# Five dense products by Strassen's scheme in a decoder layer that splits fp32 in two float32r parts

## The chip, the cores and the metric

The kernel runs on one core of one Trainium2 chip, as one launch. The metric is the device time of a run in microseconds (us). TensorE is called PE, VectorE DVE, ScalarE ACT, GpSimd POOL; SP issues most of the loads. Each engine takes its instructions from a queue of its own, in order: one that waits holds up all that stand behind it.

## What is computed

One layer for 512 tokens of width 1024. A combined input projection feeds two groups of heads, an SSD scan and a retention; their outputs go through one output projection, and a norm, a cross-attention into 256 memory tokens and a gated feed-forward part follow. Cut to the products that the change touches:

```
z, xbc, dt, q, k, v, g = split(x @ w_in)           # v: 1024 -> 1024
y_ret = silu(g) * groupnorm(retention(q, k, v))
y_ssd = rmsnorm(ssd(xbc, dt) * silu(z))
x1 = LN(alpha * x  + concat(y_ssd, y_ret) @ w_mix_out)   # 2048 -> 1024
x2 = LN(alpha * x1 + cross_attention(x1, mem))
a, u = split(causal_conv(x2 @ w_ffn_up + b))
y = LN(alpha * x2 + (silu(a) * u) @ w_ffn_down)          # 2752 -> 1024
```

## The kernel before

**Numbers.** Every fp32 operand is split in two float32r parts: h is a cast, l is the rest. A product of two tiles is three matmuls, h·h, h·l and l·h (`mm3`, line 104), which add into one bank of PSUM (128x512). The side of the tokens is kept split in SBUF; the weights come as a stream.

**The stream of weights.** `Stream` hands out 157 groups of 128x1024 in the order of their use. For each, SP loads `raw` (L124), ACT casts it to `wh` (L126) and DVE subtracts to get `wl` (L128); for 12 groups (60 to 67 and 92 to 95, `POOL_L`) POOL does the subtraction. Four pairs of `wh` and `wl` and three `raw` are in rotation, so a group is made ready while those ahead of it are used.

**The dense products.** `tok` makes 512 tokens x 512 columns: four banks, one for each 128 tokens, and each group of weights serves 24 matmuls (2 blocks of 128 rows, 4 token tiles, 3 matmuls). A product of 1024 x 1024 is two such calls, 8 groups, 192 matmuls. `feat` makes the transposed form, 128 columns x 512 tokens, also 24 matmuls to a group.

**What sets the order.** PE's instructions are pinned in the order in which the code writes them (`pin`). Small work (the chunks of the scans, norms, transposes) is written as generators that yield, and `weave` puts a few dense matmuls between its steps. The instructions of the other engines are ordered by a scheduler when the kernel is built.

**Places that the change touches.**
- The input stage: products for q, k and v; each q or k bank is turned by `rotary` (DVE multiplies at L275 and L276, POOL adds at L280 and L281). The chain for dt (`dt_chain`) is woven in.
- The gates: eight `feat` products give the retention's gate (`gate`), then two `tok` products give z (`z_gate`), where POOL multiplies (L626), takes the root of the norm (L629 to L631) and DVE scales (L632) the SSD output X[t].
- Output projection: first the retention half, with the transposes of X[t] (`ssd_out`, L108) woven in, then the SSD half, with the first norm behind it. `into_acc` adds each bank to the accumulator `acc` (L649, L651), which four POOL DMAs (L642) load with x.
- Feed-forward: tiles i of 128 columns; a pair of tiles gives one block k of the hidden product (L906), which ACT and DVE split (L908, L909). After tiles 16, 32 and 43 a part of the down projection follows: k 0 to 7, 8 to 15, then the rest.

SBUF holds tiles in several pools: `s` (20 slots of 4 KB a partition), `x`, `acc` and `row`.

Of the kernel before, what the change touches and what calls it, by code (L numbers as in the profile page):

```python
# [13 lines left out]
P = 128  # L14
T = 512
# [32 lines left out]
# columns of the parameter array  # L48
# [5 lines left out]
def tile_layer(ctx, tc, wst, wdt, xt, xn, memt, rows, small_row, par, cst, mdec, out):  # L54
# [38 lines left out]
    # The tensor engine runs its instructions in the order in which they are written here.  # L93
# [9 lines left out]
    def mmul(o, lhsT, rhs, start=True, stop=True):  # L103
        pin(nc.tensor.matmul(o, lhsT=lhsT, rhs=rhs, start=start, stop=stop))  # L104
# [6 lines left out]
    class Stream:  # L111
        def __init__(self):
            self.n = 0
            self.i = 0
            self.q = []
            self.total = wst.shape[0]

        def push(self, parts=1, between=None):
            r = ring.tile([P, 1024], F32, tag="raw", name=nm("raw"), bufs=RAW)
            h = ring.tile([P, 1024], F32R, tag="wh", name=nm("wh"))  # L120
            l = ring.tile([P, 1024], F32R, tag="wl", name=nm("wl"))
            for i in range(parts):
# [33 lines left out]
    def mm3(o, a, b, start, stop):  # L156
        mmul(o, a[0], b[0], start, False)
        mmul(o, a[0], b[1], False, False)
        mmul(o, a[1], b[0], False, stop)
# [28 lines left out]

    def drain(*gens):
        for g in gens:  # L190
            for _ in g:
                pass
# [9 lines left out]

# [1 line left out]
    xT = [slot("x", [P, 4, T], F32R) for _ in range(4)]  # L204

    def xk(k):
        return xT[k // 4][:, k % 4, :], xT[2 + k // 4][:, k % 4, :]
# [5 lines left out]
    for j in range(4):  # L213
        r = big([P, 1024])
        rv = r.rearrange("p (k t) -> p k t", k=2)
        xv = xt[j].rearrange("p (k t) -> p k t", k=2)
        h = xT[j // 2][:, 2 * (j % 2):2 * (j % 2) + 2, :]
        l = xT[2 + j // 2][:, 2 * (j % 2):2 * (j % 2) + 2, :]
# [32 lines left out]
    def bcast_row(src):  # L251
        r = slot("row", [P, 1024], F32, 2)
# [31 lines left out]
    def v_done(n):  # L284
        def done(t, b):
            (nc.scalar.copy if t % 2 else nc.vector.tensor_copy)(out=V[t][:, n * 512:(n + 1) * 512], in_=b)
        return done
# [20 lines left out]
    def dt_chain():  # L308
# [40 lines left out]
        # The differences of the running sums between two positions come from the tensor engine.  # L349
        # Four heads take 32 rows: the sums in two parts against ones, and ones against minus the sums.  # L350
# [6 lines left out]
        w = slot("acc", [P, 2, 512], F32R)  # L357
# [6 lines left out]
    dense = seq(tok(x_lhs, all8, NT, rotary(1)), *[tok(x_lhs, all8, NT, v_done(n)) for n in range(2)])  # L364
# [4 lines left out]
    maskdec = slot("row", [P, 8, P], F32, 2)  # L369
# [140 lines left out]
    def prepare(c):  # L510
        xdt = slot("acc", [P, 1024], F32)
# [8 lines left out]
    def ssd():  # L520
# [4 lines left out]
        for c in range(NT):  # L525
# [3 lines left out]
            if c < NT - 1:  # L529
                xde = slot("acc", [P, 1024], F32)  # L530
# [10 lines left out]
            def seg(q):  # L541
# [4 lines left out]
                # at or before a position the difference is at most 0; the others fall to cb's mask  # L546
# [58 lines left out]

    yret = [None] * 8

    def gate(j):
        def done(b):
# [4 lines left out]
            stt(out=sg, in0=sg, scalar=0.5, in1=y, op0=mult, op1=mult)  # L614
            yr = big([P, 2, T], F32R)
            nc.scalar.copy(out=yr[:, 0, :], in_=sg)
            tt(out=yr[:, 1, :], in0=sg, in1=f(yr[:, 0, :]), op=sub)
            yret[j] = yr
        return done

# [16 lines left out]
    drain(dense)  # L637
    drain(tok(x_lhs, all8, NT, z_gate(1)))

    acc = [slot("acc", [P, 1024], F32) for _ in range(NT)]  # L640
# [12 lines left out]

# [55 lines left out]
    def ssd_lhs(k, t):  # L709
        return yssd[t][:, 0, k, :], yssd[t][:, 1, k, :]  # L710
# [366 lines left out]
```

## Time and profile before

| | |
|---|---|
| median of 3 runs | 956.35 us (956.29 to 956.6) |
| span of the profiled execution | 953.9 us, 11550 instructions |
| its own time | the span is what the profile gives of it; 956.35 − 953.9 = 2.45 us of the median lie outside a span |
| PE | 944.3 us busy, 99% of the span |
| DVE | 563.6 us, 59% |
| ACT | 340.9 us, 36% |
| POOL | 140.0 us, 15% |
| chain of work that ended last | PE 97%, of it the dense matmuls (L104) 95% of the span and the transposes (L108) 3% |

The page is read from two sides. The busy shares say which engine has no room; the chain of work that ended last says whether that engine also sets the end, or whether it waits for others in between. Here both name PE. Durations of matmuls in a timeline are those of pipelined work (0.39 us for one of 128x512, though a new one starts each 0.23 us), so the pace is read from the distance of starts. The granted clock of TensorE is 1.00 in nearly the whole span, which is its upper level, 2.4 GHz; the lower is 1.2 GHz.

### The profile page before, as it was taken

Reading aid. Unit: us, or ns where it says so; the run is one execution under the profiler, and the core shown is the slowest. Engines: PE = TensorE matmul, PEld = TensorE weight load, DVE = VectorE, ACT = ScalarE, POOL = GpSimd, SP = SyncE. Lnnn points to the kernel's source line nnn. Section 1 sums busy time; section 2 is a strip of 40 time slices with the busy share of each in tenths; the row PEclk is TensorE's granted clock in tenths of the full one; section 3 lists DMA queues with packets and bytes.
Section 4 is the critical chain, followed back from the end, with each engine's and each line's share of the span. In section 5 each row is a group of like instructions: output and inputs, shape, how many; then the busy total and the mean of one; then the engine's idle time right before and its main releaser. Section 6 shows DMA issues by size and latency. Waiting matters only on the chain.

```text
span 953.9 us, 11550 instructions
## 1 busy us (share of the span) xinstructions
PE 944.3 (99%) x4607; PEld 776.5 (81%) x4607; DVE 563.6 (59%) x847; ACT 340.9 (36%) x487; POOL 140.0 (15%) x150
## 2 busy tenths in 40 slices
PE   9999999999999999999999999999999999999996
PEld 6788877788777888889888888988888888888874
DVE  5652566687765463448645668766535566336577
ACT  4122333345443431223533413544323443224420
POOL 1330110014252530065000006000000000000003
PEclk9999999999999999999999999999999999999999
DMA  8233211222211262425621112432322323323202
GB/s 296 87 115 103 67 45 67 67 89 67 67 45 67 89 221 88 154 89 176 221 88 47 67 66 89 136 108 88 98 101 89 111 89 95 103 89 110 89 22 89
DMA packets 26981, 95.24 MB, mean 100 GB/s; under 512 B 3120, under 2 KB 3632, under 8 KB 26928
## 3 DMA queue, kind: packets, MB, share of 16 engines
q1 hardware_dynamic: 25056, 88.09, 27.7%
q0 software_dynamic: 1728, 6.29, 1.9%
q8 instruction: 36, 0.59, 0.3%
q14 instruction: 17, 0.14, 0.1%
q10 hardware_dynamic: 144, 0.13, 0.0%
HBM read 92.41 MB, written 2.10 MB: 99 GB/s over the span
## 4 chain that ended last, share of the span: by engine, by line
PE 97%; DVE 1%; DMA 1%; SPq 0%; issue 0%; ACT 0%; DVEq 0%
PE b L104 95%; PE b L108 3%; DMA raw<-in_wst 1%; DVE acc L699 0%; DVE acc L692 0%; DVE x L153 0%; SPq L221 0%; DVE wl L128 0%; DVE acc L857 0%; DVE st L687 0%; ACT wh L126 0%; SPq L124 0%; DVEq L1073 0%; DVE st L688 0%
## 5 line engine op out<-in xcount | busy, mean ns | idle before, releaser
L104 PE MATMUL b<-x,wh 128*128 128x512 f32 (+1 forms) x1200 | 359.1, 382 | 0.5 <-DVE x L153 0.5
L128 DVE TENSOR_TENSOR wl<-raw,wh 128x1024 fp32r<-128x1024 f32 (+1 forms) x146 | 179.9, 1234 | 225.9 <-ACT wh L126 225.3
L126 ACT CAST wh<-raw 128x1024 fp32r<-128x1024 f32 (+1 forms) x157 | 164.8, 1050 | 311.5 <-PE b L104 275.1
L104 PEld LDWEIGHTS b<-x,wh 128*128 128x128 f32 x1200 | 218.2, 188 | 45.0 <-issue 4.2
L104 PE MATMUL b<-x,wl 128*128 128x512 f32 (+1 forms) x600 | 227.1, 378 | 0.0
L104 PE MATMUL b<-wh,s 128*128 128x512 f32 (+2 forms) x680 | 214.1, 391 | 0.0
L104 PE MATMUL b<-wh,x 128*128 128x512 f32 x512 | 163.2, 395 | 0.0
L104 PEld LDWEIGHTS b<-wh,s 128*128 128x128 f32 (+1 forms) x680 | 127.3, 188 | 30.7 <-issue 5.1
L104 PE MATMUL b<-wl,s 128*128 128x512 f32 (+1 forms) x340 | 131.5, 387 | 0.0
L104 PEld LDWEIGHTS b<-x,wl 128*128 128x128 f32 x600 | 112.9, 188 | 21.3
L104 PEld LDWEIGHTS b<-wh,x 128*128 128x128 f32 x512 | 96.0, 188 | 23.6 <-issue 2.2
L104 PE MATMUL b<-wl,x 128*128 128x512 f32 x256 | 99.9, 390 | 0.7 <-DVE wl L128 0.7
L104 PEld LDWEIGHTS b<-wl,s 128*128 128x128 f32 x340 | 63.9, 188 | 12.2
L257 POOL TENSOR_TENSOR st<-st,epst 128x1 f32<-128x1 f32 (+1 forms) x16 | 3.1, 192 | 479.6 <-DVE st L688 479.2
L894 DVE SCALAR_TENSOR_TENSOR t<-b,pr,t 128x511 f32<-128x511 f32 x86 | 64.1, 746 | 1.4
L104 PEld LDWEIGHTS b<-wl,x 128*128 128x128 f32 x256 | 48.1, 188 | 11.4 <-DVE wl L128 1.1
L128 POOL TENSOR_TENSOR wl<-raw,wh 128x1024 fp32r<-128x1024 f32 x12 | 34.8, 2916 | 68.5 <-ACT wh L126 68.5
L892 ACT ACTIVATE t<-b,cw,pr 128x512 f32<-128x512 f32 x43 | 33.3, 775 | 0.0
L908 ACT CAST s<-t 128x512 fp32r<-128x512 f32 (+1 forms) x22 | 13.6, 620 | 54.3 <-DVE t L906 54.3
L897 ACT ACTIVATE t<-t 128x512 f32<-128x512 f32 x21 | 13.3, 632 | 42.2 <-DVE t L895 42.2
L649 DVE TENSOR_TENSOR acc<-acc,b 128x512 f32<-128x512 f32 x24 | 15.8, 678 | 17.9 <-PE b L104 17.9
L104 PE MATMUL b<-s,wh 128*128 128x256 f32 x128 | 23.4, 285 | 0.0
(166 smaller groups left out, 856.3 us busy)
## 6 DMA issues: line engine op xcount, KB each, us to landing
raw<-in_wst SPq DMA_DIRECT2D x156, 512.0 KB, 3.3
row<-in_rows POOLq DMA_DIRECT2D x7, 512.0 KB, 6.2
acc<-in_xn POOLq DMA_DIRECT2D x4, 512.0 KB, 6.4
s<-in_xt SPq DMA_DIRECT2D x3, 512.0 KB, 7.7
out_y<-acc SPq DMA_DIRECT2D x3, 512.0 KB, 2.6
raw<-in_memt SPq DMA_DIRECT2D x2, 512.0 KB, 3.3
raw<-in_wst SPq DMA_DIRECT2D x2, 256.0 KB, 3.3
s<-in_xt SPq DMA_DIRECT2D x2, 256.0 KB, 4.3
```

The costliest lines, as they stand in the source:

```text
L104: pin(nc.tensor.matmul(o, lhsT=lhsT, rhs=rhs, start=start, stop=stop))
L108: pin(nc.tensor.transpose(o, i, ident[:p, :p]))
L126: copy(out=h[:, c], in_=r[:, c])
L128: sub_l(out=l[:, c], in0=r[:, c], in1=f(h[:, c]), op=sub)
L257: gtt(out=o, in0=v, in1=epst[:, :n], op=add)
L649: tt(out=a, in0=a, in1=b, op=add)
L892: nc.scalar.activation(out=c, in_=u, func=AF.Identity, bias=cw[0][:, i:i + 1], scale=ffp[:, i, 2:3])
L894: stt(out=c[:, d:], in0=u[:, :T - d], scalar=ffp[:, i, 2 - d:3 - d], in1=c[:, d:], op0=mult, op1=add)
L897: nc.scalar.activation(out=c, in_=c, func=AF.Silu)
L908: nc.scalar.copy(out=hd[:n, 0, :], in_=ca[:n, :])
```

## The change

Five products of 1024 x 1024 become Strassen's scheme (in Winograd's form): the values of the retention, the two halves of the output projection, and the down projection for k 0 to 7 and k 8 to 15. Tokens, inner blocks and columns are halved; instead of eight products of quarters there are seven, in the order m1, m2, m6, m5, m7, m3, m4. Each takes two groups of weights and 24 matmuls.

- **Weights.** `Quarters` has 8 loaded blocks (11, 12, 21, 22, two of each) and 14 groups to split: 11, 21, T2, T1, T3, 22, T4. The T's are sums of quarters, which POOL makes: 8 adds of 128x1024 a product (L172 to L175). Each group then serves 12 matmuls, not 24. The quarters are loaded into `s` tiles, up to 4 groups further ahead, and not before PE has reached the place of that `get`.
- **Tokens.** `sides` makes S1 to S4 with 8 POOL adds of 128x512 a product (L303; 4 of 128x1024 for the SSD half) and splits them (ACT L297, DVE L298).
- **Sums of the result.** m1, m6, m7 and m4 add up in the same two banks (`u`), m5 and m3 in two others; `done` adds a bank to `acc` after every product: 14 adds of 128x512, not 8. A bank that goes on must have been read first.
- **Moved.** `ssd_out` yields 2 ahead of its first transposes, not 4. The down projection's parts come after tiles 18, 34 and 43. `gate` no longer splits its output, `ff_done` no longer splits blocks k 0 to 15; `sides` does.
- All SBUF tiles of 4 KB come from one set `s` with 37 slots. The weights are laid out by quarters on the host.

The core of the diff:

```diff
+        ORDER = ("11", "21", "T2", "T1", "T3", "22", "T4")
+        def load(self):
+            for q in {"11": ("11",), "21": ("21",), "T2": ("12", "22")}.get(self.what, ()):
+                t = big([P, 1024])
+                d = nc.sync.dma_start(out=t, in_=wst[self.of.n + self.PLACE[q + self.k]])
+                tc.add_manual_dep(d.ins, last_pe[0].ins.name, ..., reason="not before its time")
...
+            if self.what == "T2":
+                t2_ = raw_slot()
+                add_(out=b11, in0=b12, in1=b11, op=sub)
+                add_(out=t2_, in0=b22, in1=b11, op=sub)
+                add_(out=b21, in0=b21, in1=t2_, op=sub)
+                add_(out=b12, in0=b22, in1=b12, op=sub)
...
+            h, l = pair()
+            nc.scalar.copy(out=h, in_=src)
+            tt(out=l, in0=src, in1=f(h), op=sub)
...
+    def strassen(side, done):
+        bk = {}
+        for m, a, where, start in ((1, "11", "u", True), (2, "12", "b", True), (6, "S2", "u", False),
+                                   (5, "S1", "c", True), (7, "S3", "u", False), (3, "S4", "c", False),
+                                   (4, "22", "u", False)):
+            if start:
+                bk[where] = [bank() for _ in range(2)]
+            for kp in range(2):
+                wh, wl = W.get(2)
+                for t in range(2):
+                    for j in range(2):
+                        k = 2 * kp + j
+                        mm3(bk[where][t], side(a, k, t), (wh[:, j, :], wl[:, j, :]), start and k == 0, k == 3, not start)
+                    if kp == 1:
+                        done(m, t, bk[where][t])
+                    yield
...
+        comb(a22, a21, a22, add)
+        comb(a21, a11, a21, sub)
+        comb(a11, a22, a11, sub)
+        split("S2", a11)
+        split("S1", a22)
+        comb(a12, a12, a11, sub)
+        split("S3", a21)
+        split("S4", a12)
...
-    dense = seq(*[tok(tok2(yret), all8, NT, into_acc(n, ALPHA)) for n in range(2)])
+    dense = strassen(ret_side, acc_quarter(ALPHA))
...
-    for i1, ks in ((16, list(range(8))), (32, list(range(8, 16))), (43, [16, 17])):
+    for n, i1 in enumerate((18, 34, 43)):
...
+        if n < 2:
+            drain(strassen(hid_side[n], acc_quarter(None if n else ALPHA)))
```

Three places show how the order moves. **POOL where the retention half of the output projection begins**, before: the second `z_gate` product's multiplies (L626) follow the small ones of the first.

```order
L631 TENSOR_SCALAR st_2439<-st_2439 128x1
L629 TENSOR_SCALAR st_2456<-st_2455 128x1
L630 TENSOR_TENSOR st_2456<-st_2456,mhalf 128x1
L631 TENSOR_SCALAR st_2456<-st_2456 128x1
L626 TENSOR_TENSOR s_793<-s_793,t_443_2568 128x512
L626 TENSOR_TENSOR s_794<-s_794,t_446_2585 128x512
L629 TENSOR_SCALAR st_2573<-st_2572 128x1
L630 TENSOR_TENSOR st_2573<-st_2573,mhalf 128x1
```

After: three of the eight side sums (L303, of 128x2x256) and the T2 sums of the first weights (L172 to L175) stand there; `s_843` is X[0], whose multiply is now L775.

```order
L303 TENSOR_TENSOR s_837<-s_837,s_836 128x2x256
L303 TENSOR_TENSOR s_838<-s_839,s_838 128x2x256
L303 TENSOR_TENSOR s_839<-s_839,s_838 128x2x256
L172 TENSOR_TENSOR s_2288<-s_2580,s_2288 128x1024
L173 TENSOR_TENSOR raw_2758<-s_2582,s_2288 128x1024
L175 TENSOR_TENSOR s_2580<-s_2582,s_2580 128x1024
L174 TENSOR_TENSOR s_2413<-s_2413,raw_2758 128x1024
L775 TENSOR_TENSOR s_843<-s_843,t_478_2654 128x512
L172 TENSOR_TENSOR s_2344<-s_2612,s_2344 128x1024
L778 TENSOR_SCALAR st_2659<-st_2658 128x1
L775 TENSOR_TENSOR s_844<-s_844,t_481_2671 128x512
L779 TENSOR_TENSOR st_2659<-st_2659,mhalf 128x1
```

Twelve big adds now stand ahead of the first multiply of X[0]'s second half, and two more ahead of the root (L778 to L780) that X[0] needs behind it.

**POOL between the rotary sums of q and those of k**, before (L280, L281 the rotary sums, L341 a step of the chain for dt):

```order
L280 TENSOR_TENSOR s_150<-t_50_291,t_51_292 128x8x32
L281 TENSOR_TENSOR s_150<-t_51_292,t_50_291 128x8x32
L341 TENSOR_TENSOR t_63_378<-av,cs 128x512
L280 TENSOR_TENSOR s_147<-t_73_464,t_74_465 128x8x32
L281 TENSOR_TENSOR s_147<-t_74_465,t_73_464 128x8x32
L280 TENSOR_TENSOR s_148<-t_75_476,t_76_477 128x8x32
L281 TENSOR_TENSOR s_148<-t_76_477,t_75_476 128x8x32
```

After (L424 and L425 are the rotary sums, L488 is the step for dt):

```order
L424 TENSOR_TENSOR s_154<-t_57_301,t_58_302 128x8x32
L425 TENSOR_TENSOR s_154<-t_58_302,t_57_301 128x8x32
L172 TENSOR_TENSOR s_187<-s_436,s_187 128x1024
L173 TENSOR_TENSOR raw_591<-s_438,s_187 128x1024
L175 TENSOR_TENSOR s_436<-s_438,s_436 128x1024
L488 TENSOR_TENSOR t_79_422<-av,cs 128x512
L172 TENSOR_TENSOR s_219<-s_468,s_219 128x1024
L173 TENSOR_TENSOR raw_616<-s_470,s_219 128x1024
L175 TENSOR_TENSOR s_468<-s_470,s_468 128x1024
L174 TENSOR_TENSOR s_251<-s_251,raw_591 128x1024
L424 TENSOR_TENSOR s_151<-t_90_510,t_91_511 128x8x32
```

Seven T adds for the values' weights stand between them now, and eight side sums ahead of q's.

**DVE at the last hidden block ahead of the first down part**, before (L906 the hidden product, L909 its split, L128 weight splits):

```order
L895 TENSOR_TENSOR t_905_5453<-t_905_5453,fix 128x2
L906 TENSOR_TENSOR t_900_5416<-t_900_5416,t_905_5453 128x512
L909 TENSOR_TENSOR s_5459<-t_900_5416,s_5459 128x512
L128 TENSOR_TENSOR wl_5498<-raw_5496,wh_5497 128x1024
L128 TENSOR_TENSOR wl_5528<-raw_5526,wh_5527 128x1024
```

After (L1072 the hidden product, L298 splits of side sums, L181 a weight split):

```order
L1057 TENSOR_TENSOR t_983_5614<-t_983_5614,fix 128x2
L298 TENSOR_TENSOR s_5645<-s_5101,s_5644 128x512
L1072 TENSOR_TENSOR s_5540<-t_977_5575,t_983_5614 128x512
L298 TENSOR_TENSOR s_5651<-s_5385,s_5650 128x512
L298 TENSOR_TENSOR s_5659<-s_5101,s_5658 128x512
L298 TENSOR_TENSOR s_5627<-s_5540,s_5626 128x512
L298 TENSOR_TENSOR s_5633<-s_5540,s_5632 128x512
L298 TENSOR_TENSOR s_5665<-s_5385,s_5664 128x512
L1056 SCALAR_TENSOR_TENSOR t_1003_5703<-b_5678,pr,t_1003_5703 128x511
L181 TENSOR_TENSOR wl_5710<-s_5502,wh_5709 128x1024
```

The split of a side sum, the first L298 here, stands ahead of the hidden product, and six such splits ahead of the next weight split.

## Rows read from the trace of the kernel before

**Rows 1.** The page: busy time of the engines, and the chain that ended last.
```profile
PE 944.3 (99%) x4607; PEld 776.5 (81%) x4607; DVE 563.6 (59%) x847; ACT 340.9 (36%) x487; POOL 140.0 (15%) x150
...
PE 97%; DVE 1%; DMA 1%; SPq 0%; issue 0%; ACT 0%; DVEq 0%
```

**Rows 2.** Timeline of ACT, 389 to 402 us (start, us, engine, line).
```profile
389.59 1.05 ACT L126 CAST wh<-raw 128x1024 fp32r<-128x1024 f32 x1 [4.38 <-PE b L104]
...
395.03 1.05 ACT L126 CAST wh<-raw 128x1024 fp32r<-128x1024 f32 x1 [3.43 <-PE b L104]
```

**Rows 3.** Groups by line and shape, all engines (count | busy us, mean ns | idle before).
```profile
L128 DVE TENSOR_TENSOR wl<-raw,wh 128x1024 fp32r<-128x1024 f32 x144 | 178.5, 1242 | 225.3 <-ACT wh L126 224.7
L126 ACT CAST wh<-raw 128x1024 fp32r<-128x1024 f32 x156 | 164.2, 1053 | 307.9 <-PE b L104 275.1 <-DMA raw<-in_wst 21.7 <-issue 6.2
...
L651 DVE SCALAR_TENSOR_TENSOR acc<-acc,b 128x512 f32<-128x512 f32 x24 | 16.1, 684 | 6.2 <-PE b L104 6.2
...
L909 DVE TENSOR_TENSOR s<-t,s 128x512 fp32r<-128x512 f32 x21 | 14.5, 692 | 13.0 <-ACT s L908 13.0
```

**Rows 4.** Timeline of POOL, 405 to 430 us.
```profile
407.04 2.39 POOL L128 TENSOR_TENSOR wl<-raw,wh 128x1024 fp32r<-128x1024 f32 x1 [61.79 <-ACT wh L126]
...
423.35 6.22 POOL L128 TENSOR_TENSOR wl<-raw,wh 128x1024 fp32r<-128x1024 f32 x2 [0.22 <-ACT wh L126]
```

**Rows 5.** Timeline of DVE, 422 to 431 us.
```profile
422.70 1.28 DVE L699 SCALAR_TENSOR_TENSOR acc<-acc,st,row 128x1024 f32<-128x1024 f32 x1
423.89 3.43 DVE L692 SCALAR_TENSOR_TENSOR acc<-acc,st,row 128x1024 f32<-128x1024 f32 x1
427.25 0.68 DVE L687 BATCH_NORM_STATS2 st<-acc 128x6 f32<-128x512 f32 x1
427.85 2.81 DVE L699 SCALAR_TENSOR_TENSOR acc<-acc,st,row 128x1024 f32<-128x1024 f32 x1
```

**Rows 6.** Timeline of POOL, 15 to 61 us.
```profile
19.02 0.30 POOL L881 TENSOR_TENSOR cw<-cw,pr 128x43 f32<-128x43 f32 x1
...
30.73 1.74 POOL L281 TENSOR_TENSOR s<-t,t 128x256 f32<-128x256 f32 x1
...
53.11 0.74 POOL L280 TENSOR_TENSOR s<-t,t 128x256 f32<-128x256 f32 x1 [8.20 <-DVE t L276]
```

**Rows 7.** Timeline of DVE, 29 to 31 us.
```profile
30.06 0.68 DVE L276 TENSOR_TENSOR t<-b,cs 128x512 f32<-128x512 f32 x1
30.66 1.21 DVE L128 TENSOR_TENSOR wl<-raw,wh 128x1024 fp32r<-128x1024 f32 x1
```

**Rows 8.** Timeline of POOL, 304 to 345 us.
```profile
312.80 1.28 POOL L626 TENSOR_TENSOR s<-s,t 128x512 f32<-128x512 f32 x1
...
315.74 2.19 POOL L626 TENSOR_TENSOR s<-s,t 128x512 f32<-128x512 f32 x1 [1.47 <-DVE t L603]
...
337.04 2.20 POOL L626 TENSOR_TENSOR s<-s,t 128x512 f32<-128x512 f32 x1 [1.47 <-DVE t L603]
...
342.02 2.20 POOL L642 DMA_DIRECT2D acc<-in_xn  x4
```

**Rows 9.** Timeline of DVE, 336 to 339 us.
```profile
336.87 1.22 DVE L128 TENSOR_TENSOR wl<-raw,wh 128x1024 fp32r<-128x1024 f32 x1
```

**Rows 10.** Timeline of PE, 330 to 337 us.
```profile
331.35 0.39 PE L104 MATMUL b<-wh,s 128*128 128x512 f32 x1
...
336.80 0.38 PE L108 MATMUL b<-cs,s 128*128 128x128 f32 x2
```

**Rows 11.** Landing of the acc loads (line L642, us to landing).
```profile
DMA to landing us min/median/max: 3.6/6.4/10.0
```

**Rows 12.** Timeline of PE, first 6 us.
```profile
1.18 4.02 PE L149 MATMUL b<-t 128*128 128x512 bf16 x9 [1.18 <-DVE t L146]
```

**Rows 13.** Windows after the last matmul (PE, PEld, DVE, ACT, POOL busy, PEclk, DMA, GB/s).
```profile
947.00:949.00 2.00, 0.00 (x0) 0.00 (x0) 1.90 (x5) 0.00 (x0) 0.97 (x2) 1.00 0.60 244
951.00:952.00 1.00, 0.00 (x0) 0.00 (x0) 0.00 (x0) 0.00 (x0) 0.00 (x0) 0.50 1.02 361
```

More of the change, by code (lines that the diff above doesn't have):

```diff
@@ L189, in drain, with by_pairs, raw @@
+    def by_pairs(r):
+        def raw(i, j):
+            return [r[2 * j + n][:, :, 256 * i:256 * i + 256] for n in range(2)]
+        return raw
     def drain(*gens):
@@ L282, in rotary, with v_quarter @@
         return done
[L284 to L287, printed above, removed]
+    def v_quarter(m, t, b):
+        t0, n, first = GOES[m]
+        v = V[t0 + t][:, n * 512:(n + 1) * 512]
+        if first:
+            nc.scalar.copy(out=v, in_=b)
+        else:
+            tt(out=v, in0=v, in1=b, op=add)
     all8 = list(range(KD))
@@ L356, in dt_chain @@
         tt(out=cl, in0=b, in1=f(ch), op=sub)
-        w = slot("acc", [P, 2, 512], F32R)
+        w = big([P, 2, 512], F32R)
         for i in range(2):
@@ L362, in dt_chain, with x_quarter, k_and_v @@
         seg_w.append(w)
-    dense = seq(tok(x_lhs, all8, NT, rotary(1)), *[tok(x_lhs, all8, NT, v_done(n)) for n in range(2)])
+    def x_quarter(i, j):
+        return lambda k, t: x_lhs(4 * j + k, 2 * i + t)
+    def k_and_v():
+        yield from tok(x_lhs, all8, NT, rotary(1))
+        yield from strassen(x_side, v_quarter)
+    x_side = sides(by_pairs(x_raw), gtt, {"11": x_quarter(0, 0), "12": x_quarter(0, 1), "22": x_quarter(1, 1)})
+    dense = k_and_v()
     weave(dt_chain(), dense)
     drain(dense)
-    maskdec = slot("row", [P, 8, P], F32, 2)
+    maskdec = big([P, 8, P])
     tc.keep_in_program_order(nc.gpsimd.dma_start(out=maskdec, in_=mdec))
@@ L510, in prepare @@
     def prepare(c):
-        xdt = slot("acc", [P, 1024], F32)
+        xdt = big([P, 1024])
         o = tt(out=hv(xdt), in0=hv(X[c]), in1=col(dt, c), op=mult)
@@ L637, in tile_layer @@
     drain(dense)
+    ret_side = sides(by_pairs([YT[0], YT[2], YT[1], YT[3]]), gtt)
     drain(tok(x_lhs, all8, NT, z_gate(1)))
-    acc = [slot("acc", [P, 1024], F32) for _ in range(NT)]
+    acc = [big([P, 1024]) for _ in range(NT)]
     for t in range(NT):
@@ L652, in into_acc, with acc_quarter, done @@
         return done
+    def acc_quarter(scale=None):
+        def done(m, t, b):
+            t0, n, first = GOES[m]
+            into_acc(n, scale if first else None)(t0 + t, b)
+        return done
     def tok2(tiles):
@@ L752, in v_mem @@
         return done
-    xT = [slot("x", [P, 4, T], F32R) for _ in range(4)]
+    xT = new_x()
     def first_norm():
@@ L860, in tile_layer @@
     gs = [W.get(2) for _ in range(4)]
-    xT = [slot("x", [P, 4, T], F32R) for _ in range(4)]
+    xT = new_x()
     for t in range(NT):
```

212 lines of the change are left out of this document (145 added, 67 removed).

## The prediction

> **What bounds the kernel now.** I read the page's busy times first, then the chain that ended last [rows 1]: PE is busy 944.3 of 953.9 us and 97% of the chain is PE. So whatever takes matmuls away is worth its full price, and whatever makes PE wait costs its full price; there is no slack in between. The pace comes from the ACT timeline [rows 2]: one weight group is cast each 5.44 us, the time in which PE uses a group with 24 matmuls, so 0.2267 us a matmul. Then come the engines that feed PE. The groups by line [rows 3] give a weight split on DVE 1.24 us, a side split of 512 columns 0.69, an add into the accumulator 0.68, and a weight cast on ACT 1.05. The POOL timeline [rows 4, 8] gives its big ops when DVE leaves them alone: 2.39 us for 128x1024, 1.28 for 128x512.
>
> Last, what POOL and DVE do beside each other, since the change sends them both much work on SBUF. At 423.35 POOL began two subtractions that took 6.22 us together in place of 4.78 [rows 4]; beside them two DVE ops that read two SBUF tiles took 3.43 and 2.81 us, where the one ahead of them took 1.28, and an op with one tile took its usual 0.68 between them [rows 5]. At 30.73 a POOL add took 1.74 in place of the 0.74 of its like, beside a DVE weight split of 1.21 from 30.66, while the DVE op ahead of that, which reads PSUM, took its usual 0.68 [rows 6, 7]. At 337.04 a POOL multiply took 2.20 in place of 1.28, beside a DVE split from 336.87 to 338.09: 338.09 + 1.28 is 339.37, it ended at 339.24 [rows 8, 9]. Each row reads as if one of the two waits until the other is through. So I add up POOL's big ops and the DVE ops with two SBUF inputs as if they were one queue. The Trainium skill has this as a rule, in "SBUF — State Buffer", section "Who interferes with whom": a DVE instruction with two SBUF inputs and a GpSimd instruction that reads SBUF exclude each other, and the second blocks until the first is through. The trace agrees, by the four rows named; without the rule the sum below would come out at rival B's time.
>
> **What the change removes.** Five products go from 192 to 168 matmuls: 5 × 24 × 0.2267 = **−27.2 us**, all on the path. By that alone the span would be 926.7. A product lasts 168 × 0.2267 = 38.1 us.
>
> **What it adds, a product.** POOL: 8 T adds × 2.39 = 19.1 and 8 side sums × 1.28 = 10.2, 29.3 us. DVE with two SBUF inputs: 14 weight splits × 1.24 = 17.4 and 14 side splits × 0.69 = 9.7, 27.1 us. Either alone fits beside 38.1 us of PE; as one queue they are 56.4, 18.3 too many, and the part that lies ahead of the product meets other work. The 6 more adds into the accumulator (0.68 each) read PSUM and fit on DVE. ACT gets 6 more casts of 1.05 and side casts of about the DVE split's length a product, some 15 us; with 36% busy I cost them at nothing. PE would wait for the casts if they stood behind a blocked one in ACT's queue; that is in the terms below. SP's loads are as many as before (177 in all), earlier by up to 4 groups: nothing.
>
> Whether a wait arises is a question of place, so I go through the products with PE's time of before and add up what stands in POOL's queue up to the op that PE needs.
>
> *Values.* POOL is free from 19.3 [rows 6]. Up to rotary k's first sum it has 8 side sums (10.2), 8 rotary sums of q (5.9) and 7 T adds (16.7): done at 52.1, and the sum is wanted at 53.1 [rows 6]. Alone it fits. In that stretch DVE has some 7 weight splits (8.7) and 8 side splits (5.5), 14.2 us, so it comes 13 late; rotary's temporaries then stay taken, DVE's next rotary multiply waits, and the weight splits stand behind it. The step for dt in the middle of the T adds waits for its chain too. Bounds 0 (the two queues go freely) and 17 (with the dt chain behind); I take **14**.
>
> *Retention half.* The last multiply of the first `z_gate` ends on POOL at 317.9 [rows 8]. From there to the root that X[0] needs, POOL has 8 side sums (10.2), 6 T adds (14.3) and 2 multiplies (2.6): 345.0, and some small ops between. PE starts this product at 331.35 [rows 10] and now wants X[0] after one group, at 334.1: 11 late, when DVE's 8 side splits (5.5), 5 weight splits (6.2) and its scale of X[0] are not in the way, and **24** when they are. Behind it stand the DMAs of `acc`: two multiplies and two T adds more (7.3) and a landing of 6.4 [rows 11], against 8.2 us of matmuls until m6 wants the bank `u` that only an add into `acc` frees: **5**. At the product's end the SSD half's four side sums of 1024 (9.6) wait for the last transposes, and DVE's split of S2, ahead of retention's last weight splits in its queue, waits for them: 0 to 9.6, I take **7**. Together 36 (bounds 16 and 40).
>
> *SSD half.* m6 wants T2 after 10.9 us of PE. By then POOL has 6 T adds (14.3): 3.4 late alone, 10.8 with six weight splits between (7.4). I take **10**.
>
> *Down projection, twice.* T2's quarters are loaded three groups ahead of the product, so POOL starts some 3.5 us into that tile (a load lands, a margin of mine). Up to the T2 of m6's second group it has 6 T adds and 8 side sums, 24.5: at 28.0, and the split is wanted at 3 × 5.44 + 10.9 + 2.7 = 29.9. Alone it fits, but DVE's side split stands ahead of the hidden product and of the weight splits and waits for POOL's sum: 5 to 9. With 14 side splits (9.7), 9 weight splits (11.2) and 2 products (1.4) in the same stretch it is 22.3 more: 28.0 + 22.3 − 29.9 = **20.4**, of which part is already met at the splits ahead. Twice 40.8 (bounds 10 and 44).
>
> **Sum.** 953.9 − 27.2 + 14 + 36 + 10 + 40.8 = **1027.5**, and with the 2.5 by which the median of before stands above its span, **1030 us**, 7.7% slower. I take the ends with exclusion since four rows show it and no row shows two such ops side by side at their usual lengths. With the lower and upper bounds of the terms it is 958 to 1041.
>
> **Rivals.** *B: the engines overlap freely.* Then only the queue order counts: values 2, retention half 11 + 5 + 7 = 23, up to 26 with the small ops, SSD half 3.4, down 2 × 7: 953.9 − 27.2 + 2 + 25 + 3.4 + 14 = 971, about **974 us** (955 to 1000). The side sums read strided halves, a form that no row shows, so I can't exclude it. *C: the saving arrives.* What decides is the wait of PE for X[0]: if POOL begins its side sums when each pair of gates is done, during the first `z_gate` product, it has 21.8 us more and the T adds lie behind X[0]'s multiplies in effect. Then that wait is 0 to 5, the `acc` loads come in time, and with 5 to 15 for the rest it ends at 932 to 947 of span, about **942 us**. The decision point is a sum of waits under 27.2. Against it: the side sums stand behind the last multiply of the first `z_gate` in POOL's order, which before ran at 315.74 [rows 8]. *D: the clock falls in the waits.* The first matmuls of the kernel came at 4.02 / 9 = 0.447 us each [rows 12], the lower of the two levels, 1.2 GHz, and after PE's last work the granted clock was 1.00 at first and 0.50 in the window from 951 to 952 [rows 13]. Each long wait then adds about what the start lost, 9 × (0.447 − 0.227) = 2.0 us; ten of them make 20, so **1050 us**. The Trainium skill, "TensorE: Matmul & The Clock Gate", section "What's actually happening", says so of idle stretches: TensorE falls back to 1.2 GHz and has to be busy again before it rises; in before PE never waited long enough to show it but at the end. *E: it does not do what it says*: fewer matmuls, but PE at the pace of its smaller groups, so that saving and waits cancel: within 0.2% of before, **956**.
>
> **How the numbers follow.** A 0.60 (1015 to 1041), B 0.21, C 0.09, D 0.07, E 0.03. The time is A's, 1030. For 8 in 10 the range leaves out C, E and the lower end of B, together some 0.16, and the end of D above 1055: **965 to 1055**. A measurement of this kernel can tell 0.2% (1.9 us) from no change; by that, faster 0.09 (C), the same 0.03 (E), slower 0.88.
>
> **What would show it.** Right: PE some 917 us busy in a span above 1000; waits of PE of over 10 us at the transposes (L106) early in the retention half, released by DVE's scale (L781) and that by POOL's small ops; T adds (L172 to L175) with means near 3 us and weight splits (L181) well above 1.24; the down products with waits of 5 to 12 us at their first groups and at m6. Wrong: L181 at 1.24 and L172 at 2.4 beside each other point to B; PE waits under 27 us in sum, to C; a granted clock well under 1.00 in the windows behind the waits, to D. The single weakest step is the down projection, where the same wait may be counted at several splits.

## The result, and the profile after

| | before | after |
|---|---|---|
| median | 956.37 us (956.29 to 956.6, 4 runs) | 1038.6 us (1036.92 to 1040.8, 4 runs) |
| ratio | | 1.086, 95% interval 1.0845 to 1.0876 |
| span of the profiled execution | 953.9 us | 1038.8 us |

The kernel became 8.6% slower; 1030 us with a range of 965 to 1055 had been forecast. The page of the changed kernel, busy times and the chain that ended last, answers to [rows 1]:

```profile
span 1038.8 us, 11645 instructions
...
PE 950.6 (92%) x4487; PEld 773.9 (74%) x4487; DVE 725.6 (70%) x944; ACT 393.6 (38%) x570; POOL 315.1 (30%) x226
...
PE 67%; POOL 14%; DVE 9%; issue 5%; DMA 3%; ACT 1%; SPq 0%; DVEq 0%; POOLq 0%; ACTq 0%
```

PE has fallen from 97% of the chain to 67%; POOL and DVE hold 23%, where they had 1%. PE's own waits, by what released them (total us, times, longest us):

```profile
PE b L102 <- DVE wl L181: 32.3, 11, 7.1
PE b L106 <- DVE s L781: 22.3, 1, 22.3
PE b L102 <- DVE s L801: 9.2, 2, 7.0
...
PE b L102 <- DVE s L221: 3.6, 3, 1.9
```

One wait alone is 22.3 us: the transposes of X[0] (L106) for DVE's scale (L781). The groups by line and shape (count | busy us, mean ns) answer to [rows 3, 4]:

```profile
L181 DVE TENSOR_TENSOR wl<-s,wh 128x1024 fp32r<-128x1024 f32 x60 | 90.8, 1522 | 18.6 <-ACT wh L180 18.6
L298 DVE TENSOR_TENSOR s<-s,s 128x512 fp32r<-128x512 f32 x50 | 66.7, 1384 | 11.0 <-ACT s L297 11.0
...
L303 POOL TENSOR_TENSOR s<-s,s 128x512 f32<-128x512 f32 x24 | 38.1, 1590 | 8.4 <-DVE s L298 7.3
...
L799 DVE TENSOR_TENSOR s<-s,b 128x512 f32<-128x512 f32 x48 | 31.1, 678 | 2.4 <-PE b L102 2.3
...
L175 POOL TENSOR_TENSOR s<-s,s 128x1024 f32<-128x1024 f32 x10 | 28.2, 2823 | 0.0
```

The same subtraction that took DVE 1.24 us a weight group takes 1.52 in the Strassen products (L181), a side split 1.38 in place of 0.69 (L298), a POOL side sum 1.59 in place of 1.28 (L303), a T sum up to 2.82 in place of 2.39 (L175). The add into the accumulator, which reads PSUM, is at its 0.68 (L799). That is the pattern of two engines that wait for each other.

The place of the longest wait shows how. POOL, then DVE, then PE there, three timelines of the changed kernel (start, us, engine, line):

```profile
341.49 2.84 POOL L172 TENSOR_TENSOR s<-s,s 128x1024 f32<-128x1024 f32 x1
344.41 2.67 POOL L173 TENSOR_TENSOR raw<-s,s 128x1024 f32<-128x1024 f32 x1
347.04 2.78 POOL L175 TENSOR_TENSOR s<-s,s 128x1024 f32<-128x1024 f32 x1
354.58 2.34 POOL L174 TENSOR_TENSOR s<-s,raw 128x1024 f32<-128x1024 f32 x1 [4.76 <-issue]
...
364.88 0.24 POOL L780 TENSOR_SCALAR st<-st 128x1 f32<-128x1 f32 x1
```

```profile
340.31 11.87 DVE L298 TENSOR_TENSOR s<-s,s 128x512 fp32r<-128x512 f32 x7
352.10 2.34 DVE L181 TENSOR_TENSOR wl<-s,wh 128x1024 fp32r<-128x1024 f32 x2
...
365.15 0.77 DVE L781 SCALAR_TENSOR_TENSOR s<-s,st,s 128x512 f32<-128x512 f32 x1 [5.05 <-POOL st L780]
```

```profile
343.07 0.60 PE L106 MATMUL b<-cs,s 128*128 128x128 f32 x4
365.98 0.90 PE L106 MATMUL b<-cs,s 128*128 128x128 f32 x3 [22.32 <-DVE s L781]
```

Seven side splits on DVE take 11.87 us, 4.8 at their usual length, while POOL makes T sums of 2.7 to 2.8 us. Then POOL's fourth T sum (L174) waits 4.8 us. The profile names no releaser for this wait; by the program L174 overwrites a weight tile whose split stands behind those side splits in DVE's queue, and it starts at 354.58, just behind the two splits that DVE began at 352.10. Only behind it come the two multiplies of X[0] (L775, from 356.88), two T sums of the second group (L172, L173), the root and its reciprocal (L778 to L780, through at 365.12), and DVE's scale. PE's transposes start at 365.98.

**Where the time is lost, by stage.** The start of the same operation in both traces gives the shift; the matmuls saved are added back to get what the stage lost.

| stage, up to | before | after | shift in the stage | saved matmuls | lost | taken in the prediction |
|---|---|---|---|---|---|---|
| values: first copy of the retention core (ACT) | 100.55 | 108.11 | +7.6 | 5.4 | 13.0 | 14 |
| output projection: first maximum of the cross-attention (DVE) | 486.89 | 537.07 | +42.6 | 10.9 | 53.5 | 36 + 10 |
| cross-attention: first step of the feed-forward part (ACT) | 603.37 | 656.34 | +2.8 | 0 | 2.8 | 0 |
| down product 1: convolution of tile 19 (ACT) | 742.44 | 811.31 | +15.9 | 5.4 | 21.3 | 20.4 |
| down product 2: end of the last matmul | 946.68 | 1031.59 | +16.0 | 5.4 | 21.5 | 20.4 |
| sum | | | +84.9 | 27.2 | 112.1 | 100.8 |

By another cut: PE's pauses of over 0.25 us add up to 80.8 us, against 2.4 before. In stretches at the lower clock level PE was busy for 58 us; at twice the clock that is an estimated 29. Together 107.6 of the 112. The windows show the level (us, busy of PE, PEld, DVE, ACT, POOL, then PEclk):

```profile
100.00:340.00 240.00, 239.13 (x1219) 189.37 (x1217) 156.11 (x264) 95.52 (x155) 63.14 (x62) 1.00 0.23 77
340.00:440.00 100.00, 60.80 (x250) 48.10 (x251) 76.04 (x60) 40.48 (x56) 65.66 (x42) 0.83 0.26 85
745.00:775.00 30.00, 17.24 (x41) 11.85 (x40) 26.83 (x25) 10.90 (x15) 20.40 (x9) 0.60 0.25 87
```

Whether those 29 us are a loss of their own is the question of one experiment below.

### The profile page after: what moved, and what is told of

It is laid out like the page before. It is cut to its first block, busy times and chain, and to the rows that moved or that the text cites. A ratio compares the mean times of both kernels' runs of the same rounds, so it can differ in the third digit from the quotient of the medians.

```text
span 1038.8 us, 11645 instructions
## 1 busy us (share of the span) xinstructions
PE 950.6 (92%) x4487; PEld 773.9 (74%) x4487; DVE 725.6 (70%) x944; ACT 393.6 (38%) x570; POOL 315.1 (30%) x226
## 4 chain that ended last, share of the span: by engine, by line
PE 67%; POOL 14%; DVE 9%; issue 5%; DMA 3%; ACT 1%; SPq 0%; DVEq 0%; POOLq 0%; ACTq 0%
PE b L102 65%; POOL s L303 5%; DVE s L298 3%; DVE wl L181 2%; PE b L106 2%; POOL s L175 1%; POOL wl L133 1%; POOL raw L173 1%; DMA s<-in_wst 1%; POOL s L172 1%; POOL s L775 1%; POOL st L779 1%; DMA pr<-in_par 1%; DMA s<-in_xn 1%; ACT s L297 1%
## 5 line engine op out<-in xcount | busy, mean ns | idle before, releaser
L102 PE MATMUL b<-wh,s 128*128 128x512 f32 (+2 forms) x1112 | 371.9, 410 | 19.7 <-DVE s L801 9.2
L102 PE MATMUL b<-s,wh 128*128 128x512 f32 (+1 forms) x1328 | 385.4, 375 | 3.6 <-DVE s L221 3.6
L102 PEld LDWEIGHTS b<-wh,s 128*128 128x128 f32 (+1 forms) x1112 | 219.9, 198 | 78.8 <-issue 14.2
L102 PEld LDWEIGHTS b<-s,wh 128*128 128x128 f32 x1328 | 240.6, 191 | 48.4 <-issue 4.4
L102 PE MATMUL b<-wl,s 128*128 128x512 f32 (+2 forms) x556 | 227.0, 408 | 32.3 <-DVE wl L181 32.3
L102 PE MATMUL b<-s,wl 128*128 128x512 f32 (+1 forms) x664 | 246.6, 371 | 0.0
L102 PEld LDWEIGHTS b<-wl,s 128*128 128x128 f32 (+1 forms) x556 | 110.7, 199 | 58.9 <-DVE wl L181 36.4
L102 PEld LDWEIGHTS b<-s,wl 128*128 128x128 f32 x664 | 126.6, 191 | 21.5
L181 DVE TENSOR_TENSOR wl<-s,wh 128x1024 fp32r<-128x1024 f32 x60 | 90.8, 1522 | 18.6 <-ACT wh L180 18.6
L180 ACT CAST wh<-s 128x1024 fp32r<-128x1024 f32 x60 | 62.6, 1050 | 84.8 <-PE b L102 80.5
L172 POOL TENSOR_TENSOR s<-s,s 128x1024 f32<-128x1024 f32 x10 | 27.0, 2698 | 200.5 <-DVE t L1057 186.4
L298 DVE TENSOR_TENSOR s<-s,s 128x512 fp32r<-128x512 f32 (+1 forms) x57 | 76.3, 1385 | 15.7 <-ACT s L297 15.7
L303 POOL TENSOR_TENSOR s<-s,s 128x512 f32<-128x512 f32 (+1 forms) x28 | 49.4, 1766 | 23.7 <-DVE s L298 22.4
L297 ACT CAST s<-s 128x512 fp32r<-128x512 f32 (+1 forms) x57 | 35.4, 669 | 50.1 <-POOL s L303 48.4
L220 ACT CAST s<-b 128x256 fp32r<-128x256 f32 (+1 forms) x56 | 24.7, 470 | 54.9 <-PE b L106 22.3
L106 PE MATMUL b<-cs,s 128*128 128x128 f32 x136 | 18.4, 278 | 22.3 <-DVE s L781 22.3
```

Of the source, the lines that this page charges most:

```text
L106: pin(nc.tensor.transpose(o, i, ident[:p, :p]))
L172: add_(out=b11, in0=b12, in1=b11, op=sub)
L180: nc.scalar.copy(out=h, in_=src)
L181: tt(out=l, in0=src, in1=f(h), op=sub)
L297: nc.scalar.copy(out=h[:, c, :], in_=x)
L298: tt(out=l[:, c, :], in0=x, in1=f(h[:, c, :]), op=sub)
```

## The experiments

Theory 1: POOL's ops that read SBUF and DVE's ops with two SBUF inputs exclude each other, so the two engines work off a product's sums and splits as one queue. Theory 2: they overlap freely, and the waits come from the order of the queues and from the load of each engine alone. A third account, a clock that falls in the waits, was open beside both.

### Two POOL ops beside the splits, in the kernel before

```diff
             drain(feat(xk, T, ff_done(i)))
+            if 16 <= i < 32:
+                for _ in range(2):
+                    gtt(out=dum, in0=dum, in1=dum, op=sub)   # not before PE is here
```

> The kernel before with two POOL subtractions of 128x1024 more after each of the feed-forward tiles 16 to 31; nobody waits for their result. Theory 1: where they run, weight splits on DVE (L128) take 1.7 to 2.4 us in the mean in place of 1.24 and POOL's own op about 3 in place of 2.39, while DVE's convolution steps (L894, one input in PSUM) stay at 0.75; DVE has room, so the time stays within 956 to 965. Theory 2: L128 at 1.24 and POOL at 2.39.

Measured: 956.4 us in one run, beside 956.33 for the kernel before. The groups on DVE in the stretch with the added ops, 725.9 to 812 us:

```profile
L128 DVE TENSOR_TENSOR wl<-raw,wh 128x1024 fp32r<-128x1024 f32 x16 | 23.7, 1483 | 17.6 <-ACT wh L126 17.6
L909 DVE TENSOR_TENSOR s<-t,s 128x512 fp32r<-128x512 f32 x7 | 11.4, 1631 | 4.8 <-ACT s L908 4.8
...
L894 DVE SCALAR_TENSOR_TENSOR t<-b,pr,t 128x511 f32<-128x511 f32 x15 | 11.1, 737 | 0.0
L895 DVE TENSOR_TENSOR t<-t,fix 128x2 f32<-128x2 f32 x15 | 7.8, 518 | 0.0
```

A piece of its timeline:

```profile
734.27 1.52 DVE L894 SCALAR_TENSOR_TENSOR t<-b,pr,t 128x511 f32<-128x511 f32 x2
...
736.81 4.20 POOL L941 TENSOR_TENSOR dum<-dum 128x1024 f32<-128x1024 f32 x2 [0.71 <-PE b L104]
...
737.53 1.72 DVE L909 TENSOR_TENSOR s<-t,s 128x512 fp32r<-128x512 f32 x1 [0.69 <-ACT s L908]
...
739.18 2.91 DVE L128 TENSOR_TENSOR wl<-raw,wh 128x1024 fp32r<-128x1024 f32 x1
...
747.69 4.39 POOL L941 TENSOR_TENSOR dum<-dum 128x1024 f32<-128x1024 f32 x2 [1.58 <-PE b L104]
748.56 1.04 DVE L895 TENSOR_TENSOR t<-t,fix 128x2 f32<-128x2 f32 x1
```

The split of a hidden block took 1.72 us in place of 0.69 and a weight split 2.91 in place of 1.23, while the convolution steps (L894), with one input in PSUM, stayed at 0.74 to 0.76 right beside a POOL op. In the mean over the stretch L128 rose from 1.23 to 1.48 and L909 from 0.69 to 1.63. The clearest rows are those of the smallest op: the fix-up of two columns (L895, two SBUF inputs) has 0.15 us of work, and in all 15 cases here it ended 0.01 to 0.02 us after a POOL op did, however long that took. The one above, of 1.04 us, ended at 749.60; the first of POOL's two ops ended at 749.58. For L128 1.7 to 2.4 had been expected. All 16 met a POOL op, but only three met it in its course (2.04 to 2.91 us). Seven met only its end (1.33), and six began first and kept their 1.21, while the POOL op behind them took 2.4 in place of 1.89; for POOL about 3 had been expected. Nobody waited for the added ops, so the time did not move: the exclusion is there, but costs only where there is no room for it.

### All sums on DVE

```diff
-            add_ = gtt if self.of.pool else tt
+            add_ = tt
...
-                adds(out=o_, in0=x0, in1=x1, op=op)
+                tt(out=o_, in0=x0, in1=x1, op=op)
```

> The changed kernel with all T sums and side sums on DVE in place of POOL. Theory 1 (POOL's big ops and DVE's ops with two SBUF inputs exclude each other): DVE's queue then holds a product's 27.1 us of splits and 8 x 1.24 + 8 x 0.69 = 15.4 us of sums, 42.5 in place of the 56.4 of both engines, and no op waits for the other engine; weight splits (L181) back at 1.24 us, waits and clock together 30 to 50 us in place of 112: 957 to 980 us. Theory 2 (the engines overlap freely, the waits come from the order of queues and from a DVE that is nearly full): DVE gets 15 us more in each product of 38 us, 36.6 + 15.4 = 52 us with the adds into the accumulator, and the kernel becomes slower than 1039: 1050 to 1080 us.

Measured: 987.72 us, ratio to the kernel before 1.0336 (1.0307 to 1.0365). Groups by line of this kernel:

```profile
L181 DVE TENSOR_TENSOR wl<-s,wh 128x1024 fp32r<-128x1024 f32 x60 | 72.6, 1219 | 19.8 <-ACT wh L180 19.7
...
L298 DVE TENSOR_TENSOR s<-s,s 128x512 fp32r<-128x512 f32 x50 | 35.5, 756 | 0.0
...
L175 DVE TENSOR_TENSOR s<-s,s 128x1024 f32<-128x1024 f32 x10 | 12.2, 1217 | 0.0
```

Its busy times:

```profile
PE 935.4 (95%) x4487; PEld 763.8 (78%) x4487; DVE 707.3 (72%) x1020; ACT 393.5 (40%) x570; POOL 144.9 (15%) x150
```

DVE got 15 us more work a product, and the kernel became 51 us faster than the changed one. That decides against theory 2 as it was priced, which had it slower. DVE's busy time even fell, from 725.6 to 707.3 us, though it now has 76 more ops: waiting inside the old ones is gone. It does not decide against a third reading, that POOL alone is too slow for these sums; the run without DVE's splits below bears on that. Splits are back at 1.22 and 0.76, and a T sum costs DVE 1.22 where it cost POOL 2.39 and more. It stayed 8 us above the expected range; the windows of the two stages that still lose (DVE is the third figure) point to DVE itself:

```profile
318.00:440.00 122.00, 102.88 (x432) 82.50 (x431) 107.31 (x120) 54.33 (x71) 24.49 (x34) 0.92 0.28 97
690.00:735.00 45.00, 38.54 (x161) 30.65 (x160) 42.95 (x61) 20.81 (x30) 0.00 (x0) 0.96 0.24 84
```

DVE is busy 107.3 of 122 us in the output projection and 43.0 of 45 at the first down product. By the starts of the same operations the values' stage came out 0.9 us ahead of the kernel before, the output projection fell 21.6 us behind it and the down products 3.5 and 4.1. That a full DVE causes these losses is argued from the busy share and not shown by a run.

### One kind of sums on DVE

T sums on DVE and side sums on POOL; then the reverse. Each is one half of the diff above.

> The changed kernel with the T sums (128x1024) on DVE, the side sums left on POOL. Theory 1 as one queue of both engines: 10.2 (POOL side sums) + 27.1 + 9.9 = 47.2 us a product, between 42.5 (all on DVE, 987.7 us) and 56.4 (1038.6): by a straight line 987.7 + 4.7 x 3.66 = 1005 us. Theory 2 (each engine's own load): DVE has 46.5 with the adds into the accumulator and POOL 10.2, so no slower than all on DVE: 975 to 990.

Measured: 1002.02 us, one run.

> The changed kernel with the side sums on DVE, the T sums left on POOL. Theory 1 as one queue: 19.1 + 27.1 + 5.5 = 51.7 us a product: by the same line 987.7 + 9.2 x 3.66 = 1021 us. Theory 2: DVE has 42 and POOL 19.1, both near 38 or below: 965 to 985.

Measured: 1016.61 us, one run. With the two ends this makes a row of four, against the work of a product added up over both engines:

| sums on | both engines as one queue, us a product | measured, us |
|---|---|---|
| DVE, both kinds | 42.5 | 987.7 |
| DVE the T sums, POOL the side sums | 47.2 | 1002.0 |
| POOL the T sums, DVE the side sums | 51.7 | 1016.6 |
| POOL, both kinds | 56.4 | 1038.6 |

The straight line had said 1005 and 1021, the loads of each engine alone 975 to 990 and 965 to 985. The sum over both engines orders all four and gives the size. So does POOL's own load, though: with 0, 10.2, 19.1 and 29.3 us of sums on POOL a straight line gives 1005 and 1021 as well, since a sum costs DVE about half of what it costs POOL. The row of four rules out theory 2 as it was priced, and cannot tell one queue from a POOL that is too slow by itself. Nor does each single wait follow the sum: that for X[0] is 13.0 us with the side sums on POOL and 4.4 with the T sums there.

### POOL's sums without DVE's splits

```diff
             h, l = pair()
             nc.scalar.copy(out=h, in_=src)
-            tt(out=l, in0=src, in1=f(h), op=sub)
-            return h, l
+            return h, h
```

and the same in `sides`.

> The changed kernel with all sums on POOL, but DVE's subtractions of the Strassen products left out (side splits L298 and weight splits L181; the h part stands in for the l part in the matmuls, whose number stays). Theory 1 (exclusion): POOL's sums have DVE's ops hardly beside them and go at 2.4 and 1.3 us; the wait for X[0] falls from 22.3 to the 11 to 14 us that POOL's queue takes by itself, the down products lose nearly all of their waits: 945 to 975 us. Theory 2 (POOL's own queue is the wait, DVE has no part in it): X[0] waits 20 us or more as before, 1015 us or more.

Measured: 978.37 us, one run. Its waits on PE, and the groups of two kinds of sums on POOL:

```profile
PE b L106 <- DVE s L779: 10.2, 1, 10.2
PE b L102 <- ACT wh L180: 7.4, 2, 3.7
```

```profile
L301 POOL TENSOR_TENSOR s<-s,s 128x512 f32<-128x512 f32 x24 | 34.6, 1442 | 4.2 <-ACT s L296 3.5
...
L172 POOL TENSOR_TENSOR s<-s,s 128x1024 f32<-128x1024 f32 x10 | 24.0, 2399 | 197.8 <-DMA s<-in_wst 187.0 <-ACT wh L180 10.7
```

The wait for X[0] fell from 22.3 to 10.2 us (11 was the prediction's figure for POOL's queue by itself), and the T sums went at 2.4 to 2.5. The values' stage lost 0.4 us in place of 13.0. POOL has the same sums to make as in the changed kernel, so POOL's load alone does not give the 1038.6. The fall of the wait mixes two effects, however: POOL's ops are no longer held up, and the 4.8 us for which L174 waited behind DVE's side splits are gone with those splits. The time is 3 us above the expected range: the output projection lost 30.2 us, and the down products 9.1 and 8.8 (shifts of +3.7 and +3.4), with the weight casts of ACT (L180) as the longest wait, behind the casts of side sums that wait for POOL. That part is the order of the queues, as rival B had it (7 us each).

### No sums at all

The T sums and side sums are left out; the plain quarters stand in for them.

```diff
-                add_(out=b11, in0=b12, in1=b11, op=sub)   # and the three others
-                src = t2_
+                src = b22
...
         def comb(o, v0, v1, op):
-            for o_, x0, x1 in zip(o, v0, v1):
-                adds(out=o_, in0=x0, in1=x1, op=op)
+            pass
```

> The changed kernel with the T sums and side sums left out (the plain quarters are split and multiplied in their place; matmuls, splits, loads and adds into the accumulator are all there). Theory 1: without POOL's 29.3 us a product the waits go, and the 27.2 us of the 120 matmuls arrive: 930 to 940 us. Rival (the smaller groups of 12 matmuls, 14 splits and 14 adds a product hold PE up by themselves): more than half of the waits stay, 980 us or more.

Measured: 936.89 us, one run. Its largest waits on PE, and its busy times:

```profile
PE b L102 <- DVE s L217: 3.6, 3, 1.9
PE b L102 <- DVE s L796: 2.0, 1, 2.0
PE b L102 <- DVE wl L133: 1.5, 1, 1.5
...
PE 918.9 (98%) x4487; PEld 753.7 (81%) x4487; DVE 640.4 (68%) x944; ACT 394.0 (42%) x570; POOL 142.3 (15%) x150
```

So in the values and the down products the smaller groups, 14 splits and 14 adds a product hold nothing up: the last matmul ends 18.8 us earlier than before, 5.3 of it from the values and 5.4 from each down product, nearly all or the whole of 5.44. In the stage of the output projection only 3.8 of 10.9 arrive, so 7.0 us are lost there without any sum; three waits of 1.5 to 2.0 us (a weight split, an add into the accumulator, the split of the first norm) are 5.4 of them. The second norm costs 1.25 more. DVE has the same 944 ops here as in the changed kernel, and with POOL's sums gone they take 640.4 us in place of 725.6: POOL's sums beside them had made the same ops 85 us longer.

### PE kept busy in its waits

```diff
+    def turn(n):
+        o = bank()
+        for _ in range(n):
+            pin(nc.tensor.matmul(o, lhsT=warm[:, :P], rhs=warm, start=True, stop=True))
...
+            if t == 0:
+                turn(92)
             to_features(X[t], ...)
```

and `turn(28)` ahead of m6 of the retention half, `turn(12)`, `turn(28)` and `turn(9)` in each down product.

> The changed kernel with short bf16 matmuls that nobody reads in the places of PE's longest waits: 92 ahead of the first transposes of X[0], 28 ahead of m6 of the retention half, 12, 28 and 9 in each down product; 218 x 0.2235 = 48.7 us that fill waits of 22.3, 7.0 and twice 12.7. If the low clock behind the waits costs what the windows say (29 us in all, some 20 of them at these places), the time falls to 1017 to 1024. If the clock costs nothing beyond the waits, it stays at 1036 to 1042.

Measured: 1042.12 us, ratio to the kernel before 1.0898 (1.0881 to 1.0914). The upper branch of the expectation, 1036 to 1042, was passed by 0.1. The mean granted clock rose from 0.952 to 0.981, and in the first down product from 0.60 to 0.89, as this window shows beside that of the changed kernel above:

```profile
745.00:775.00 30.00, 23.05 (x91) 14.92 (x90) 26.74 (x23) 11.11 (x14) 19.39 (x9) 0.89 0.24 84
```

The time did not fall. The transposes of X[0] start at the same time as in the changed kernel, to 0.06 us:

```profile
365.92 0.55 PE L106 MATMUL b<-cs,s 128*128 128x128 f32 x3 [2.47 <-DVE s L790]
```

The work at the lower level that was saved, an estimated 29.2 − 13.4 = 15.8 us by the same count, went into longer pauses. The end of each wait is set by POOL and DVE, not by how fast PE came to it. Rival D, the clock as 20 us on top, is out for these places; the low clock is there, but in time that PE would have waited.

Where PE itself sets the end the same two traces show a price. Behind the second norm both have the same pauses (1.37 and 0.28 us), but the changed kernel ran there at the lower level for a while. These windows hold that place, first in the changed kernel, then in this run:

```profile
638.00:643.00 5.00, 4.72 (x28) 4.64 (x27) 4.90 (x6) 1.13 (x2) 5.00 (x3) 0.66 0.61 210
638.00:643.00 5.00, 4.72 (x39) 4.52 (x40) 4.90 (x8) 2.23 (x5) 5.00 (x3) 1.00 0.56 177
```

The cross-attention stage lost 2.8 us in the changed kernel and 1.25 here, so some 1.5 of the 2.8 are the clock.

### The values alone

```diff
+        x_side = sides(by_pairs(x_raw), tt, {...})      # behind the key product
         yield from strassen(x_side, v_quarter)
```

The four other products are `tok` calls again.

> Only the retention values by Strassen's scheme, its sums on DVE and its side sums written behind the key product so that the chain for dt goes ahead of them on DVE; the four other products as in the kernel before, tiles in the one set of 4 KB. With all sums on DVE the values' stage came out 0.9 us ahead of the kernel before, 4.5 of waits against 5.4 of matmuls; part of these waits were for the chain of dt (1.7 and 1.2 us). Theory 1: 24 matmuls less, 5.4 us, and 1 to 4 us of waits: 952 to 955.5 us. Rival: DVE's sums displace its other work all the same, 956 to 960.

Measured: 959.49 us (956.89 to 961.46; the traced run took 958.6), ratio 1.0029 (1.0018 to 1.0039): the rival's range. Its waits on PE:

```profile
PE b L102 <- DVE s L219: 3.3, 3, 1.7
PE b L102 <- DVE wl L181: 1.8, 1, 1.8
...
PE b L102 <- ACT wh L180: 1.2, 1, 1.2
```

The values' stage came out only 0.5 us ahead, with waits at m6 for T2's cast and split, and 1.9 and 1.3 us were lost behind the two norms, in front of the feature products. There the output of a norm is split in four pieces of 256 columns in place of two of 512 (L219), because the tiles of x are now 4 KB. The changed kernel has the same pieces; there the stretch behind the second norm is the third line of the stage table, 2.8 us with some 1.5 of low clock in it, and that behind the first lies in the second line. The prediction had both at nothing.

### The values with T1 first, and then with the down products

```diff
-        ORDER = ("11", "21", "T2", "T1", "T3", "22", "T4")
+        ORDER = ("11", "21", "T1", "T2", "T3", "22", "T4")      # each sum where its group comes
...
-        (1, ..), (2, ..), (6, "S2", "u", False), (5, "S1", "c", True), (7, ..)
+        (1, ..), (2, ..), (5, "S1", "c", True), (6, "S2", "u", False), (7, ..)
```

and x in tiles of 8 KB in a set of its own.

> The values alone, as in the run before, with two edits. The products go in the order m1, m2, m5, m6, m7, m3, m4 and the sums in the order of their use (T1 and S1, one sum each, ahead of T2 and S2), since the run before waited 1.2 and 1.8 us at m6 for T2 and lost 1.4 us to the low clock behind; and the tiles of x are of 8 KB again, in a set of their own, since the norms behind (4 splits of 256 columns in place of 2 of 512) cost 1.9 and 1.3 us. If both readings hold: 953.9 - 5.4 + 0 to 2 of waits, 950 to 954 us with what lies outside the span. If the wait only moves to the next product (DVE has 36 of 46 us there): 956 to 960.

Measured: 954.52 us, ratio 0.9979 (0.997 to 0.9988), 0.5 above the expected 950 to 954. The waits of this product that are left:

```profile
PE b L102 <- DVE wl L187: 2.6, 3, 0.9
```

> As the values with T1 first, and the two down products by Strassen's scheme with all sums on DVE in the same order. With all sums on DVE they came out 3.5 and 4.1 us behind the kernel before, 3.6 and 4.2 of it one wait at m6 for T2 and some 1.4 to 2.3 the low clock behind. If the new order takes that wait away: 949 to 953 us. If DVE is the bound there as the window says (43 of 45 us busy): the wait goes elsewhere, each product stays 3 to 5 us behind, 956 to 962 us.

Measured: 953.32 us, ratio 0.9968 (0.9955 to 0.998), the fastest of the runs that leave nothing of the layer out. Its waits for splits, and its busy times:

```profile
PE b L102 <- DVE wl L187: 8.3, 7, 1.9
```

```profile
PE 931.3 (98%) x4535; PEld 762.3 (80%) x4535; DVE 644.1 (68%) x947; ACT 369.8 (39%) x529; POOL 145.3 (15%) x150
```

The norms are back at before (shift of −0.1 us). The values keep 2.0 of their 5.4 us, the down products 0.8 and 0.2 of theirs, and neither run shows the lower clock before the last matmul. The expectation of the last run, 949 to 953, was missed by 0.3. The waits of 3.6 and 4.2 us at m6 are gone; with all sums on DVE the profile had put them down to the adds into the accumulator (L801 and L799), which stood behind T sums in DVE's queue. In their place came several of under 2 us, most of them for splits. So of 16.3 us of matmuls saved in three products some 3.1 arrive.

## Why the prediction was right

**The bound and the saving.** Right. Without the sums the last matmul ends 18.8 us earlier, and in the values and the down products nearly all of the 5.44 us arrive. In the output projection 7.0 of 10.9 are lost even without sums, which no term of the prediction held.

**POOL and DVE as one queue.** Right, and the step on which all else rested. It had been read from four rows; the added POOL ops show it directly, by ops that end with POOL's. The same 944 DVE ops take 85 us longer beside POOL's sums than without them. The four placements of the sums follow the added-up work, though POOL's load would order them as well; without DVE's splits, and with POOL's load unchanged, the time falls to 978 and the wait for X[0] to what POOL alone needs. How the 112 us divide between exclusion and order of the queues no run shows exactly, since leaving DVE's splits out takes both away. The rule of the Trainium skill ("SBUF — State Buffer", section "Who interferes with whom") agrees with these runs in both halves: ops with two SBUF inputs are held up (a weight split of 2.91 us in place of 1.23), those with one input in PSUM are not (0.74).

**The terms.** Values 14 against 13.0, down products 20.4 against 21.3 and 21.5: right in size. The wait for X[0], 24 against 22.3, the wait for bank `u` at m6, 5 against 7.0 (L801, longest). Mis-sized was the output projection as a whole, 46 taken against 53.5, its last part above all: 7 + 10 were taken for retention's end and the SSD half, and what remains of the 53.5 beside those two waits is 24. Left out were the splits behind the norms, a wait of 1.9 at the first, with sums and without, and 1.25 at the second without the low clock, an effect of the smaller tiles that I had costed at nothing by not naming it. In the down products the waits themselves were smaller than forecast, 12.8 and 13.5 us of pauses, with matmuls at the lower clock level in between; the total of the stage came out as reckoned because POOL's and DVE's work sets its end either way, as the run with PE kept busy shows (20.9 and 23.1 lost there, with the clock at 0.89 in place of 0.60 in the window of the first). The sign for PE's busy time, some 917 us, did not come: it is 950.6, with an estimated 29 us too many from the low clock.

**The rivals.** B's signs did not come: L181 is at 1.52 and L172 at 2.70, not at 1.24 and 2.4. The kernel without DVE's splits comes near B's time, 978 against 974, but DVE's load is gone there too, so it is no measurement of B. B's doubt about strided side sums is settled: in the changed kernel they take 1.29 us where DVE is idle, from 327.98 on. C's condition, waits under 27 us, was never near. D was right on the clock (0.60 in the window of a down product) and wrong on its price in the waits that were filled; behind the second norm it has one, some 1.5 us.

**What stayed open.** Why the output projection still falls 21.6 us behind with all sums on DVE was not taken apart; 7.0 of what it loses are there without sums too, DVE is busy 88% of that stretch, and no run tried its products one by one, or the loads of the accumulator on another queue.

## What to carry to other kernels

When a change trades work of the bound engine for work of its feeders, add the feeders up by what they share and not by engine: here POOL's ops on SBUF and DVE's ops with two SBUF inputs are one queue, and 56 us of it do not fit beside 38 us of matmuls, while either engine's part alone seems to. Put such sums on the engine that does them at half the price even if it is the busier one, and order them by first use. And a low clock behind a wait is a cost only where PE itself sets what comes next: look at who ends the next wait first.

## What the runs showed of the hardware that was not expected

- A DVE op of two columns waits for the end of a POOL op of 128x1024: the fix-up of the convolution (L895, two SBUF inputs) went from 0.15 us in the mean to 0.52 with POOL beside it, at most 1.04, and ended with the POOL op in 15 cases of 15.
- A POOL subtraction of 128x1024 took 1.89 us when both inputs and the output were the same tile (the added ops, at their least), 2.39 with two different inputs.
- Keeping PE busy raised the mean granted clock from 0.952 to 0.981 and did not lower the time (1042.1 us against 1038.6).
